# First layer of a two-layer hybrid transformer block: output product of head groups A and B once for all token tiles, root buffers by kind, and an FFN that opens with six blocks for the context alone

## The chip, the cores and the metric

The kernel runs on one core of a Trainium2 chip. A core has five engines that run their own instruction streams and meet at semaphores: TensorE (PE, matrix products), VectorE (DVE), ScalarE (ACT), GpSimd (POOL) and SyncE (SP, which here only issues transfers). The metric is the device time of one execution in microseconds. What can be told from no change is about 0.3%, that is 5.5 us.

## The reference

Two layers work on 256 context tokens and 256 latent tokens of width 1024. In both, a combined input product feeds three head groups (A: windowed attention, B: a state-space scan, C: differential attention), their outputs are joined and multiplied by `w_out`, and a layer norm follows; then a feed-forward network, dense in the first layer and with eight experts in the second, and another layer norm.

```python
for li in range(DEPTH):                                    # DEPTH = 2
    sh1, sc1, g1, sh2, sc2, g2 = split(c_act @ w_ada[li] + b_ada[li], 6)     # and ..c for the context
    ya, yb, yd = group_A(...), group_B(...), group_C(...)  # 384 + 384 + 256 columns
    mix = concat([ya, yb, yd], -1) @ w_out[li]
    x = post_ln(ALPHA * x + g1 * mix, ln1_g[li], ln1_b[li])
    x = post_ln(ALPHA * x + g2 * ffn(modulate(x, sh2, sc2)), ln2_g[li], ln2_b[li])
    # layer 0: the same for ctx, with the context's own sh, sc, g
# ffn of layer 0: g, u = split(h @ w_gu, 2); (silu(g) * u) @ w_down        # 1024 -> 2816 -> 1024
```

## The kernel before

The 512 tokens are four tiles of 128: tiles 0 and 1 are the context (`CTX`), 2 and 3 the latent tokens (`LAT`). Every large product is made from split operands: a weight piece `raw` is loaded (four buffers), ACT copies it into `whi` (a rounded form), and DVE or POOL subtracts to get `wlo` (three buffers each, function `split`); three products `hi*hi`, `hi*lo`, `lo*hi` are added up in one accumulator (`mm3`, lines 273, 274 and 276). Activations are split the same way into `HI` and `LO`.

In the first layer the end of attention, the output product and the start of the FFN overlap. Attention C makes for each head a pair of scores (`SC`, L919), a softmax on DVE and ACT, transposes (`PT`, L865), and a product with the values (`yC`, L932); when all heads of a tile are done DVE takes an inverse root by a chain of small instructions (`rstd_of`, L227 to L239) and scales (L942), and PE transposes the result (`py`, L952). `tail0` runs beside it. It calls `out_ab` (the columns of groups A and B times `w_out`, in four column blocks `j`, each with a weight piece of 512 KB and one of 256 KB) and `out_c` (the columns of group C), first for the context tiles and then for the latent ones, so the pieces of `out_ab` are loaded and split twice. After `out_c` of a tile come `post_ln` (L479, L480) and `layernorm` (`lnx`, L425), and for a pair of tiles `make_hT`: eight steps that transpose `lnx` (`hT`, L433) and write `HI` and `LO` of that half (L438 to L444), the input of the FFN.

Then `ada_group(L1, 0)` stands in the program: sixteen loads of 512 KB of `w_ada`, each followed by four products `ada` (L316; the profile counts two records for each) with the conditioning vector; the result is needed at the end of the FFN. It shares the four `raw` buffers. `ffn` follows: 22 column blocks in two halves; `gate_up(f, s)` loads 1 MB of weights for a block (two pieces, POOL makes the `wlo` of the first, DVE of the second) and makes 48 products `gu`, with 256 columns if `s` is one half of the tokens and with 512 if both. The first `M0` = 3 blocks run for the context half alone, then the same three for the latent half, and the other eight of the first half for both.

The order on every engine is not written out: a scheduler places each instruction, by the program's order, its dependencies and a timeline of its own, and engines then work strictly in that order. The constants of the second layer (`lcst`, L376) are loaded on SP into the buffer that the first layer's constants hold until attention C's last use of them (L935).

Of the kernel before, what the change touches and what calls it, by code (L numbers as in the profile page):

```python
# [12 lines left out]
F = mybir.dt.float32  # L13
FR = mybir.dt.float32r
BF = mybir.dt.bfloat16
I32 = mybir.dt.int32
# [15 lines left out]
FT = 22  # L32
NE = 8
BIG = 1.0e30
M0 = 3
LOP = 0, 1
KP = 1, 0
XC = 0, 4
# [76 lines left out]
def kernel(ctx: ExitStack, tc: tile.TileContext, I, out: bass.AP):  # L115
# [21 lines left out]
    def p_(tag, name):  # L137
        return ps.tile([128, 512], F, name=name, tag=tag, bufs=NBUF[tag])
# [79 lines left out]
        return (I["ctx"] if t in CTX else I["x"])[0, (t % 2) * 128:(t % 2 + 1) * 128]  # L218


    def rstd_of(v, n, scale=1.0):


        a = sm.tile([128, 3, 8], F, name="nw", tag="nw", bufs=6)
        ve, y, t = (a[:, i, :n] for i in range(3))
        iv = sm.tile([128, 2, 8], I32, name="nwi", tag="nwi", bufs=6)
        V.tensor_scalar(ve, v, scale, EPS, op0=OP.mult, op1=OP.add)  # L227
        V.tensor_scalar(iv[:, 0, :n], ve.bitcast(I32), 1, None, op0=OP.logical_shift_right)
        V.tensor_scalar(iv[:, 1, :n], iv[:, 0, :n], -1, 0x5F3759DF, op0=OP.mult, op1=OP.add)
        cur, f = iv[:, 1, :n].bitcast(F), 1.0  # L230
        for _ in range(3):
            if n == 1:
                V.scalar_tensor_tensor(t, cur, ve, cur, op0=OP.mult, op1=OP.mult)
            else:
                V.tensor_tensor(t, cur, cur, op=OP.mult)
                V.tensor_tensor(t, t, ve, op=OP.mult)
            V.scalar_tensor_tensor(y, t, 3.0 * f * f, cur, op0=OP.subtract, op1=OP.mult)
            cur, f = y, -2.0 * f ** 3
        V.tensor_scalar(y, y, 1.0 / f, None, op0=OP.mult)  # L239
        return y  # L240
# [178 lines left out]

    def layernorm(pool, xs, t):  # L420
        mu, rs = ln_stats(xs[t])
        n = pool.tile([128, D], F, name="lnx", tag="lnx", bufs=LNB if pool is lp else 4)
        nm = sm.tile([128, 1], F, name="nmr", tag="nmr")
        V.scalar_tensor_tensor(nm, mu, -1.0, rs, op0=OP.mult, op1=OP.mult)
        S.activation(n, xs[t], AF.Identity, scale=rs, bias=nm)  # L425
        return n
# [79 lines left out]
    def mixers(L, full_ctx, fill, tail):  # L506
# [326 lines left out]
        def ssd_finish(t, y):  # L833
            z = zcol(t, 0, 384)
            th = sp.tile([128, 384], F, name="zth", tag="yB", bufs=3)
            S.activation(r4(th, 3), z, AF.Tanh, scale=0.5)
            V.scalar_tensor_tensor(r4(th, 3), r4(th, 3), 1.0, z, op0=OP.add, op1=OP.mult)
            V.scalar_tensor_tensor(y, y, 0.5, th, op0=OP.mult, op1=OP.mult)
            ss = sm.tile([128, 1], F, name="ss", tag="ss")
            S.activation(th, y, AF.Square, accum_out=ss)  # L840
            rs = rstd_of(ss, 1, 1.0 / 384)
            V.scalar_tensor_tensor(y, y, rs, L.snw, op0=OP.mult, op1=OP.mult)
            put_y(t, y, 3, 3)

# [61 lines left out]
        def attn_C(t):  # L906
            n = keys(t)
            nb = n // 128
            y = mp.tile([128, 256], F, name="yC", tag="yCs", bufs=2)
            ss = sm.tile([128, 4], F, name="ssC", tag="ssC")  # L910
            for h in range(4):
                st_ = sm.tile([128, 5, 2], F, name="smx", tag="smx", bufs=6)
                l, r = st_[:, 2], st_[:, 3]
                Ps, pos = [], []
                for i in range(2):
                    po = p_("S", "SC")
                    pos.append(po)
                    b0 = 32 * ((2 * h + i) % 4)
                    T.matmul(po[:, :n], qTC(t)[b0:b0 + 32, h // 2], kTC[b0:b0 + 32, h // 2, :n], start=True,  # L919
                             stop=True)  # L920
                for i in range(2):
                    Ps.append(softmax(pos[i], n, None, 32 ** -0.5, st_, i))
                yield 0.0017 * n
                V.reciprocal(r, l)
                V.tensor_tensor(r[:, 1:2], r[:, 1:2], L.nlam, op=OP.mult)
                S.activation(Ps[1][:, :n], Ps[1][:, :n], AF.Copy, scale=r[:, 1:2])
                V.scalar_tensor_tensor(Ps[0][:, :n], Ps[0][:, :n], r[:, 0:1], Ps[1][:, :n], op0=OP.mult, op1=OP.add)
                PT = transp(Ps[0], n)
                yield 0.08 * nb
                yp = p_("y", "yC")  # L930
                for b in range(nb):
                    T.matmul(yp[:, 0:64], PT[:, b], vC[:, b, h * 64:(h + 1) * 64], start=(b == 0), stop=(b == nb - 1))  # L932
                yh = y[:, h * 64:(h + 1) * 64]
                S.activation(yh, yp[:, 0:64], AF.Square, accum_out=ss[:, h:h + 1])
                V.tensor_tensor(yh, yp[:, 0:64], L.dnw, op=OP.mult)  # L935
                yield 0.13 * nb
                if h % 2 and t in CH[li] or h == 3:
                    a = h - 1 if t in CH[li] else 0
                    n_ = h + 1 - a
                    rs = rstd_of(ss[:, a:h + 1], n_, 1.0 / 64)  # L940
                    yv = y[:, a * 64:(h + 1) * 64]
                    V.tensor_tensor(r4(yv, n_), r4(yv, n_), rs[:, :, None].to_broadcast([128, n_, 64]), op=OP.mult)  # L942
                    put_y(t, yv, 6 + a // 2, n_ // 2)
                    yield 0.2
                    yield f"+yC{t}{h // 2}"
# [181 lines left out]
            post_ln(xs[t], *L.ln1, LN1[t - 2] if L.li else None)  # L1127
            yield t

    def ffn(L, pp, done):  # L1130
        li = L.li
        xs = L.xs
        W = I["ffn_w_gu"][0].rearrange("(k p) (a n) -> p k a n", p=128, a=2)
# [3 lines left out]
        b = bc_load(L.pp, I["ln2_b"][li], L.nbc)  # L1137
        act = {}

        def gate_up(f, s):  # L1140
            wk = kpieces(lambda k0: [((slice(None), slice(None), a), W[:, k0:k0 + 4, a, f * 128:(f + 1) * 128])
                                     for a in range(2)], [128, 4, 2, 128])
            o = slice(s.start * 256, s.stop * 256)
            pg = [p_("S", "gu"), p_("mm", "gu")]
            for a in range(2):
                for k0 in range(0, KC, KG):
                    mm3(pg[a][:, o], [(wk(k)[0][:, a], wk(k)[1][:, a], HI[:, s, k], LO[:, s, k], True)
                                      for k in range(k0, k0 + KG)], k0 == 0, k0 + KG == KC)
            sl = L.pp.tile([128, 512], F, name="silu", tag="otmp", bufs=OT)
            S.activation(sl[:, o], pg[0][:, o], AF.Silu)  # L1150
            V.tensor_tensor(sl[:, o], sl[:, o], pg[1][:, o], op=OP.mult)
            if f not in act:
# [6 lines left out]
        for half in range(2):  # L1159
# [2 lines left out]

            for s in range(2):
                for f in range(f0, f0 + n0):
                    gate_up(f, slice(s, s + 1))
            for f in range(f0 + n0, f0 + 11):
                gate_up(f, slice(0, 2))
            for c, tiles in ((0, (0, 1, 2, 3)), (1, (0, 1, 2, 3))) if half == 0 else DN:
# [553 lines left out]
    def tail0():  # L1722
        yield "?S"
        pp = L0.pp = L0.tp = post.enter_context(tc.tile_pool(name="post0", bufs=1))
        out_consts(L0, range(NT), pp)
        ns = {}
        for tiles in TL0:
            yield from out_ab(L0, tiles, pp)
            for v in out_c(L0, tiles, pp):
                if type(v) is int:  # L1730
                    ns[v] = layernorm(pp, L0.xs, v)
# [10 lines left out]
                    yield v  # L1742

    mixers(L0, True, [ada_group(L0, 1), ada_group(L0, 2)], tail0())
    for _ in ada_group(L1, 0):
        pass
    with tc.tile_pool(name="ffn", bufs=1) as fp:
        ffn(L0, fp, lambda tiles: make_hT(L0.pp, L1.mod1, {t: layernorm(L0.pp, L0.xs, t) for t in tiles},
                                          tiles[0] // 2))
    post.close()  # L1750


# [61 lines left out]
```

## Time and profile before

| | us |
|---|---|
| median of 3 runs | 1819.82 (1815.51 to 1820.83) |
| the profiled execution | 1821.04 |
| its span in the trace | 1819.2 |
| PE busy in it | 1663.7 (91%) |
| DVE, ACT, POOL busy | 1154.5, 874.4, 321.9 |

The profile is of one execution. Its times count from the start of the span; 1.8 us of the execution lie around the span. A PE that is called busy need not be at full speed: the clock that the chip grants it is listed beside it, in shares of 2.4 GHz, and 0.50 is the lower level of 1.2 GHz. Idle time is put down to what ended it.

### The profile page before, as it was taken

To read this page: it belongs to the slowest core of one execution; us is meant where nothing else is said; L and a number is where in the kernel's file an instruction comes from. 1 tells how busy PE (TensorE), PEld (TensorE's weight loads), DVE (VectorE), ACT (ScalarE), POOL (GpSimd) and SP (SyncE) were. 2 spreads that over 40 slices of the span, in tenths; PEclk is the share of its full clock that TensorE was granted. 3 is DMA by queue.
4 is the path that set the end of the run, shared out by engine and by line. 5 is a ranking of instruction groups with operands and counts; after the bars stand their busy time and mean duration, and the time that the engine had idled before them with its cause. 6 is when DMAs were issued, how large, how long until landed. Compare 5 with 4: busy or idle time off the path is not lost.

```text
span 1819.2 us, 26372 instructions
## 1 busy us (share of the span) xinstructions
PE 1663.7 (91%) x9454; PEld 1244.2 (68%) x9454; DVE 1154.5 (63%) x2224; ACT 874.4 (48%) x1447; POOL 321.9 (18%) x254
## 2 busy tenths in 40 slices
PE   5898989887999999987999984899999999999995
PEld 2677657674988888876786672487686685784782
DVE  4673668658632343288587756288785586982895
ACT  3433545543622132335444652376673574772770
POOL 1221013334420022474232141000000000000000
PEclk8999998878999999999899996899999999999998
DMA  9327454328633233345676227999999999999995
GB/s 306 86 67 236 127 149 123 107 66 269 188 93 96 89 101 96 110 165 167 209 223 207 65 82 300 395 406 409 408 406 376 399 406 409 406 408 387 408 407 229
DMA packets 248153, 436.09 MB, mean 240 GB/s; under 512 B 15025, under 2 KB 166329, under 8 KB 248017
## 3 DMA queue, kind: packets, MB, share of 16 engines
q1 hardware_dynamic: 246096, 429.55, 66.2%
q0 software_dynamic: 1920, 4.81, 1.0%
q8 instruction: 76, 1.25, 0.3%
q14 instruction: 61, 0.49, 0.1%
HBM read 431.08 MB, written 3.23 MB: 239 GB/s over the span
## 4 chain that ended last, share of the span: by engine, by line
PE 77%; DMA 8%; DVE 7%; issue 2%; ACT 2%; POOL 0%; SPq 0%; ACTq 0%; DVEq 0%; POOLq 0%
PE mg L1369 6%; PE mu L1369 6%; PE mdn L1369 5%; PE gu L273 5%; PE gu L274 5%; PE gu L276 4%; DMA raw<-in_w_ada 4%; PE mu L1358 3%; PE mg L1358 3%; PE mdn L1358 3%; PE tok L276 2%; DMA mraw<-in_exp_w_gu 2%; PE ada L316 2%; PE tok L273 2%; PE SC L919 2%; PE tok L274 2%
## 5 line engine op out<-in xcount | busy, mean ns | idle before, releaser
L1349 DVE TENSOR_TENSOR mwl<-mraw,mwh 128x1024 fp32r<-128x1024 f32 (+1 forms) x350 | 389.4, 1160 | 37.2 <-ACT mwh L1348 20.2
L1348 ACT ACTIVATE mwh<-mraw 128x1024 fp32r<-128x1024 f32 (+1 forms) x350 | 337.8, 1013 | 61.4 <-PE mg L1369 22.9
L260 POOL TENSOR_TENSOR wlo<-raw,whi 128x1024 fp32r<-128x1024 f32 (+2 forms) x93 | 224.1, 2416 | 482.2 <-ACT whi L259 435.1
L259 ACT ACTIVATE whi<-raw 128x1024 fp32r<-128x1024 f32 (+2 forms) x168 | 168.2, 1004 | 237.3 <-PE dn L274 71.9
L260 DVE TENSOR_TENSOR wlo<-raw,whi 128x1024 fp32r<-128x1024 f32 (+2 forms) x75 | 90.5, 1206 | 144.1 <-ACT whi L259 142.8
L273 PE MATMUL gu<-HI,whi 128*128 128x512 f32 (+1 forms) x400 | 144.2, 369 | 2.3 <-ACT whi L259 2.3
L274 PE MATMUL gu<-LO,whi 128*128 128x512 f32 (+1 forms) x400 | 144.9, 369 | 0.0
L273 PE MATMUL tok<-whi,HI 128*128 128x256 f32 (+2 forms) x400 | 108.7, 301 | 5.4 <-ACT xin L550 4.3
L274 PE MATMUL tok<-whi,LO 128*128 128x256 f32 (+2 forms) x400 | 106.4, 295 | 5.2 <-DVE LO L444 5.1
L316 PE MATMUL ada<-raw,cT 128*32 128x256 f32 x768 | 75.5, 430 | 37.8 <-DMA raw<-in_w_ada 35.9
L276 PE MATMUL gu<-HI,wlo 128*128 128x512 f32 (+1 forms) x400 | 98.5, 368 | 0.0
L273 PEld LDWEIGHTS tok<-whi,HI 128*128 128x128 f32 x400 | 79.2, 199 | 14.9 <-issue 5.4
L273 PEld LDWEIGHTS gu<-HI,whi 128*128 128x128 f32 x400 | 75.7, 190 | 15.8 <-ACT whi L259 2.5
L274 PEld LDWEIGHTS tok<-whi,LO 128*128 128x128 f32 x400 | 79.3, 199 | 9.1 <-DVE LO L444 5.8
L274 PEld LDWEIGHTS gu<-LO,whi 128*128 128x128 f32 x400 | 76.1, 191 | 12.8
L276 PEld LDWEIGHTS gu<-HI,wlo 128*128 128x128 f32 x400 | 70.5, 189 | 12.9
L273 PE MATMUL dn<-whi,ah 128*128 128x512 f32 x176 | 70.3, 399 | 5.6 <-ACT whi L259 5.6
L276 PE MATMUL tok<-wlo,HI 128*128 128x256 f32 (+2 forms) x400 | 72.3, 299 | 1.9 <-DVE nw L227 1.9
L1369 PE MATMUL mg<-mwh,Xh 128*128 128x512 f32 x240 | 72.5, 383 | 1.7 <-ACT mwh L1348 1.6
L1369 PE MATMUL mdn<-mwh,mah 128*128 128x512 f32 x220 | 70.1, 400 | 0.9 <-ACT mwh L1348 0.9
L1369 PE MATMUL mg<-mwh,Xl 128*128 128x512 f32 x240 | 70.8, 376 | 0.0
L1369 PE MATMUL mu<-mwh,Xl 128*128 128x512 f32 x240 | 70.7, 376 | 0.0
(361 smaller groups left out, 3496.5 us busy)
## 6 DMA issues: line engine op xcount, KB each, us to landing
mraw<-in_exp_w_gu SPq DMA_DIRECT2D x128, 1024.0 KB, 15.8
mraw<-in_exp_w_down SPq DMA_DIRECT2D x88, 1024.0 KB, 15.6
mraw<-in_exp_w_gu SPq DMA_DIRECT2D x64, 768.0 KB, 13.8
raw<-in_w_ada SPq DMA_DIRECT2D x88, 512.0 KB, 4.8
raw<-in_ffn_w_gu SPq DMA_DIRECT2D x100, 256.0 KB, 3.4
raw<-in_w_in SPq DMA_DIRECT2D x38, 512.0 KB, 5.1
raw<-in_ffn_w_down SPq DMA_DIRECT2D x30, 512.0 KB, 3.7
E<-cscr POOLq DMA_DIRECT2D x12, 384.0 KB, 7.2
```

Source lines behind the costliest of these rows:

```text
L259: S.activation(hi, raw, AF.Copy)
L260: (eng or V).tensor_tensor(lo, raw, hi.bitcast(F), op=OP.subtract)
L273: T.matmul(o, ah, bh, start=start and i == 0, stop=False)
L274: T.matmul(o, *((ah, bl) if wa else (al, bh)), start=False, stop=False)
L276: T.matmul(o, *((al, bh) if wa else (ah, bl)), start=False, stop=stop and i == n - 1)
L316: T.matmul(pa[32 * j:32 * j + 32, hs], cT[:, k], w[j], start=(k == 0), stop=(k == KC - 1), tile_position=(0, 32 * j), skip_group_check=True)
L919: T.matmul(po[:, :n], qTC(t)[b0:b0 + 32, h // 2], kTC[b0:b0 + 32, h // 2, :n], start=True, stop=True)
L1348: S.activation(wh, raw, AF.Copy)
L1349: V.tensor_tensor(wl, raw, wh.bitcast(F), op=OP.subtract)
L1358: T.matmul(pc[:, :w], xh, wl[:, c * 512:c * 512 + w], start=False, stop=stop)
L1369: T.matmul(pc[:, :w], x, wh[:, c * 512:c * 512 + w], start=start and x is xh, stop=False)
```

## The change

Three parts. First, `tail0` calls `out_ab` once for all four tiles ahead of both `out_c`, so its weight pieces are loaded and split once, and no product of A or B starts before all tiles' group A and B outputs are there. Second, the buffers of the inverse roots are separate for group B, group C and the rest (three each, where six were shared); `lnx` has three buffers in place of four; the FFN's `silu` has two buffers of its own. Third, `M0` is 6, `ada_group(L1, 0)` is no longer ahead of the FFN but inside it, as `side`, after the six blocks of the context half; the half blocks take their accumulators from other tags.

```diff
-M0 = 3
+M0 = 6
...
-    def rstd_of(v, n, scale=1.0):
+    def rstd_of(v, n, scale=1.0, kind=""):
-        a = sm.tile([128, 3, 8], F, name="nw", tag="nw", bufs=6)
+        a = (lc if kind else sm).tile([128, 3, 8], F, name="nw", tag="nw" + kind, bufs=3)
-        iv = sm.tile([128, 2, 8], I32, name="nwi", tag="nwi", bufs=6)
+        iv = (lc if kind else sm).tile([128, 2, 8], I32, name="nwi", tag="nwi" + kind, bufs=3)
...
-        n = pool.tile([128, D], F, name="lnx", tag="lnx", bufs=LNB if pool is lp else 4)
+        n = pool.tile([128, D], F, name="lnx", tag="lnx", bufs=LNB if pool is lp else 3)
...
-            rs = rstd_of(ss, 1, 1.0 / 384)
+            rs = rstd_of(ss, 1, 1.0 / 384, "S")
...
-                    rs = rstd_of(ss[:, a:h + 1], n_, 1.0 / 64)
+                    rs = rstd_of(ss[:, a:h + 1], n_, 1.0 / 64, "C")
...
-        def gate_up(f, s):
+        def gate_up(f, s, tags=("S", "mm")):
-            pg = [p_("S", "gu"), p_("mm", "gu")]
+            pg = [p_(tag, "gu") for tag in tags]
...
-            sl = L.pp.tile([128, 512], F, name="silu", tag="otmp", bufs=OT)
+            sl = L.pp.tile([128, 512], F, name="silu", tag="silu", bufs=2)
...
-                    gate_up(f, slice(s, s + 1))
+                    gate_up(f, slice(s, s + 1), ("mm" if s else "S", "S"))
+                if s == 0 and half == 0:
+                    for _ in side:
+                        pass
...
+        yield from out_ab(L0, range(NT), pp)
         for tiles in TL0:
-            yield from out_ab(L0, tiles, pp)
             for v in out_c(L0, tiles, pp):
...
-    for _ in ada_group(L1, 0):
-        pass
```

Three places show how the order moves. On PE, between the last heads of attention C (tile 2, the products `yC` and the transposes `py`) and the first transposes `hT` of the FFN's input; after:

```order
L276 MATMUL op<-wlo,HI 128x512 x2
L932 MATMUL yC<-vC,PT 128x64 x4
L865 MATMUL PT<-cf,P 128x128 x8
L932 MATMUL yC<-vC,PT 128x64 x12
L952 MATMUL py<-cf,yC 128x128 x2
L433 MATMUL hT<-cf,lnx 128x128 x2
L273 MATMUL op<-whi,HI 128x512 x2
```

and before, from the same two products on:

```order
L276 MATMUL op<-wlo,HI 128x512 x2
L932 MATMUL yC<-vC,PT 128x64 x4
L865 MATMUL PT<-cf,P 128x128 x8
L273 MATMUL op<-whi,HI 128x256
L274 MATMUL op<-whi,LO 128x256
L273 MATMUL op<-whi,HI 128x256
```

The 144 products `op` of 256 columns (`out_ab` of the latent tiles) that stood between these heads' `yC` and behind them are now all further up; `ada`, which stood around `py`, is gone from here too.

On PE, the 64 products `ada`, which now follow the context half's six blocks `gu`; after:

```order
L276 MATMUL gu<-HI,wlo 128x256 x4
L316 MATMUL ada<-raw,cT 32x256 x12
L433 MATMUL hT<-cf,lnx 128x128 x2
L316 MATMUL ada<-raw,cT 32x256 x4
L433 MATMUL hT<-cf,lnx 128x128 x2
L316 MATMUL ada<-raw,cT 32x256 x16
L337 MATMUL tp<-cf,rows 128x128 x2
L316 MATMUL ada<-raw,cT 32x256 x32
L337 MATMUL tp<-cf,rows 128x128 x2
L273 MATMUL gu<-HI,whi 128x256
```

and before, the last of them, ahead of the first `gu`:

```order
L316 MATMUL ada<-raw,cT 32x256 x20
L433 MATMUL hT<-cf,lnx 128x128 x4
L316 MATMUL ada<-raw,cT 32x256 x4
L433 MATMUL hT<-cf,lnx 128x128 x2
L316 MATMUL ada<-raw,cT 32x256 x4
L433 MATMUL hT<-cf,lnx 128x128 x4
L316 MATMUL ada<-raw,cT 32x256 x8
L433 MATMUL hT<-cf,lnx 128x128 x4
L273 MATMUL gu<-HI,whi 128x256
```

They were spread over the end of the output product and the context's `hT`; now they stand in one place with two pairs of `hT` and no `gu` among them.

On SP, what is queued ahead of the second layer's constants `lcst`; after:

```order
L253 DMA raw<-in_w_out 128x2x512 x4
L253 DMA raw<-in_ffn_w_gu 128x4x128 x6
L351 DMA bc<-gscr 128x1024
L253 DMA raw<-in_ffn_w_gu 128x4x128 x4
L376 DMA lcst<-in_attn_sink 128x6
L376 DMA lcst<-in_dt_bias 128x12
```

and before:

```order
L253 DMA raw<-in_w_out 128x256
L253 DMA raw<-in_w_out 128x2x256
L253 DMA raw<-in_w_out 128x2x512 x2
L376 DMA lcst<-in_attn_sink 128x6
L376 DMA lcst<-in_dt_bias 128x12
```

Ten loads of FFN weights, five pieces, now stand between `w_out` and the constants. On DVE `lcst` (L398 to L403) stands among the instructions of tile 2's inverse root and of tile 1's layer norm, before and after.

## Rows read from the trace of the kernel before

**Rows 1.** Stretches: us, then busy us of each engine, clock, DMA share, GB/s

```profile
355.00:382.00 27.00, 21.57 (x75) 14.02 (x76) 16.93 (x68) 14.24 (x45) 4.08 (x4) 0.63 0.01 2
...
426.90:448.70 21.80, 13.78 (x113) 6.05 (x109) 18.31 (x65) 9.50 (x18) 6.03 (x6) 0.84 0.99 303
580.00:600.00 20.00, 20.00 (x88) 16.24 (x87) 4.37 (x4) 3.81 (x4) 0.00 (x0) 1.00 0.28 86
```

**Rows 2.** PE's waits, 300 to 450: who, for whom, us, times, longest

```profile
PE py L952 <- DVE yC L942: 9.2, 2, 5.5
PE ada L316 <- DMA raw<-in_w_ada: 4.7, 4, 1.6
PE op L276 <- DVE wlo L260: 3.2, 1, 3.2
```

**Rows 3.** Timeline of PE, attention C: start, us, instruction, idle before it

```profile
345.92 0.28 PE L273 MATMUL op<-whi,HI 128*128 128x256 f32 x1
346.04 0.28 PE L274 MATMUL op<-whi,LO 128*128 128x256 f32 x1
346.36 1.12 PE L919 MATMUL SC<-kTC,YT 32*128 32x512 f32 x2
...
355.02 0.88 PE L952 MATMUL py<-cf,yC 128*128 128x128 f32 x3 [5.50 <-DVE yC L942]
...
371.77 2.07 PE L919 MATMUL SC<-kTC,YT 32*128 32x512 f32 x2
...
382.00 0.88 PE L952 MATMUL py<-cf,yC 128*128 128x128 f32 x3 [3.67 <-DVE yC L942]
```

**Rows 4.** Timeline of DVE: the inverse roots of tile 1, and layer norm pieces

```profile
378.85 0.23 DVE L227 TENSOR_SCALAR nw<-ssC 128x4 f32<-128x4 f32 x2
...
381.43 0.63 DVE L942 TENSOR_TENSOR yC<-yC,nw 128x256 f32<-128x256 f32 x2
...
422.97 1.28 DVE L480 SCALAR_TENSOR_TENSOR xr<-xr,nw,bc 128x1024 f32<-128x1024 f32 x1
```

**Rows 5.** Timelines of DVE, POOL and ACT: the end of attention C

```profile
401.96 0.23 DVE L935 TENSOR_TENSOR yC<-yC,lcst 128x64 f32<-128x64 f32 x1 [0.60 <-ACT yC L934]
...
403.53 2.33 DVE L235 TENSOR_TENSOR nw<-nwi 128x4 f32<-128x4 f32 x1
...
403.42 2.42 POOL L260 TENSOR_TENSOR wlo<-raw,whi 128x1024 fp32r<-128x1024 f32 x1
...
415.85 0.36 DVE L942 TENSOR_TENSOR yC<-yC,nw 128x256 f32<-128x256 f32 x1
...
435.31 1.24 ACT L425 ACTIVATE lnx<-xr,nmr,nw 128x1024 f32<-128x1024 f32 x1 [11.03 <-DVE nmr L424]
```

**Rows 6.** Transfers issued 400 to 450: count, KB each, us to landing

```profile
raw<-in_w_ada SPq DMA_DIRECT2D x16, 512.0 KB, 5.1
...
lcst<-in_lam_k SPq DMA_DIRECT2D x1, 32.0 KB, 3.4
```

**Rows 7.** The tile lcst: who uses it, ns min/median/max, first and last start

```profile
L376 SPq DMA_DIRECT2D lcst<-in_attn_sink x1: 340/340/340, 402.2 to 402.2; - x1
...
L376 SPq DMA_DIRECT2D lcst<-in_lam_k x1: 327/327/327, 407.0 to 407.0; - x1
L398 DVE TENSOR_SCALAR lcst<-lcst x1: 159/159/159, 407.2 to 407.2; 128x6 f32<-128x6 f32 x1
```

**Rows 8.** Timelines of PE and ACT: hT, ada and the first gu

```profile
436.84 0.44 PE L433 MATMUL hT<-cf,lnx 128*128 128x128 f32 x2
...
437.20 0.56 ACT L438 ACTIVATE HI<-hT,mod 128x256 fp32r<-128x256 f32 x1 [0.65 <-PE hT L433]
437.67 0.56 ACT L440 ACTIVATE hfull<-hT,mod 128x256 f32<-128x256 f32 x1
...
443.92 1.90 PE L316 MATMUL ada<-raw,cT 128*32 128x256 f32 x16
...
448.70 0.39 PE L273 MATMUL gu<-HI,whi 128*128 128x256 f32 x1 [2.29 <-ACT whi L259]
```

More of the change, by code (lines that the diff above doesn't have):

```diff
@@ L1128, in out_c, with ffn @@
             yield t
-    def ffn(L, pp, done):
+    def ffn(L, pp, done, side):
         li = L.li
@@ L1744 @@
     mixers(L0, True, [ada_group(L0, 1), ada_group(L0, 2)], tail0())
-    for _ in ada_group(L1, 0):
-        pass
     with tc.tile_pool(name="ffn", bufs=1) as fp:
         ffn(L0, fp, lambda tiles: make_hT(L0.pp, L1.mod1, {t: layernorm(L0.pp, L0.xs, t) for t in tiles},
-                                          tiles[0] // 2))
+                                          tiles[0] // 2), ada_group(L1, 0))
     post.close()
```

## The prediction, made before the changed kernel was run

> **What bounds the kernel now.** I read the stretches first, then PE's waits, then the timelines between 345 and 449 us, where everything that the change moves lies. PE is the bound nearly everywhere: it is busy 20 of 20 us in the FFN at full clock, 88 products of 512 columns in 20 us, so 0.227 us each, and it is short of work only in the stretch from the output product to the first `gu` [rows 1]. There two things are to be seen. From 355 to 382 PE runs at 0.63 of its clock and is idle 5.4 us with the transfers all but silent (0.01); from 426.9 to 448.7 it is busy 13.8 of 21.8 us while the DMA engines are full (0.99) at 303 GB/s: that is `w_ada`. The waits say what ends last: twice the inverse root of attention C (9.2 us), four times a load of `w_ada` (4.7), once a `wlo` of the second `out_ab` (3.2) [rows 2]. So before, the loads of `w_ada` and the chain of DVE run side by side, and both hold up the FFN.
>
> **Part 1, `out_ab` once.** It takes away 3 MB of loads, eight copies on ACT and eight subtractions. PE loses nothing: the products are the same. Those loads stood in front of no one but in the wait of 3.2 us [rows 2], so the saving is that, plus the idle time that the latent products can now fill.
>
> How much of it they fill: a product of 256 columns takes 0.118 us (345.92 to 346.04) [rows 3]. In the new order 216 of the 288 products stand ahead of the first `py` of group C, against 144 before, so 72 x 0.118 = 8.5 us of work go into an idle time of 5.5 [rows 3]: the first `py` comes 3.0 later. Then 28 stand between this `py` and the next heads' `PT`, and 20 between `PT` and `yC`: 48 x 0.118 = 5.7, of which some 1.8 were spent there before, so these heads are 6.9 late. Up to the second `py` (382.0 before; I call this point P) the other 24 products lie in waits. Against that, PE should be warmer: a pair of `SC` takes 1.12 us at full clock and 2.07 at the low one, and the last idle 3.7 us before P [rows 3] were DVE's; I take 5 us back. Last, the inverse root of tile 1: 2.6 us from L227 to L942, 13 pairs of instructions by 0.2, and 0.6 for L942 itself [rows 4]. In the new order tile 0's layer norm stands among them, L480 by 1.28 [rows 4], two statistics instructions at about half that and a dozen small ones by 0.1 to 0.2: 4.5 us more. P moves from 382 to 382 + 6.9 - 5 + 4.5, 388 rounded; bounds 381 (all of the clock and of the idle time is won back) and 393 (none).
>
> From P to `hT`, the first place that the order shows. Before, it takes 54.8 us (to 436.84) [rows 8], since DVE works off the latent products' and layer norms' instructions in between and lnx of tile 1 is only made at 435.31 [rows 5]. After, PE has there 12 products of 512 columns, 16 `PT`, 16 `yC` and two `py`, some 8 us, and then waits. DVE's chain is what counts: the last L935, tile 2's inverse root, tile 1's layer norm. Among these stand the `lcst` instructions, as before, where L398 started at 407.2, just 5.0 after its load was issued [rows 7]. In the new order that load stands behind five pieces of FFN weights, and the fifth needs the buffer of the first, which POOL must have subtracted: after tile 1's products (P + 7 if the clock is low), a copy, and a queue on POOL of two subtractions by 2.42 [rows 5] and an addition, that is P + 12, about when the last L935 ends too. Then 0.7 for the two loads of that piece, 5.0 to landing, 4.8 from the first constant's issue to the last one's [rows 7], 3.4 to its landing [rows 6]: L403 at P + 21, L480 and L942 at P + 23, where it took 14.2 us from L935 to L942 before [rows 5] and takes 11 now. Tile 1's layer norm then needs 4.7 us of small instructions and lnx 1.24 [rows 5]: `hT` at P + 29.7. So `hT` comes at 388 + 29.7 = 417.7 in place of 436.8. Bounds for this stretch: 24 (the constants land before DVE gets to them) and 33.
>
> **A rule on DVE and POOL.** The row first: an L235 of four columns, 0.1 us elsewhere, took 2.33 while POOL made a `wlo` of 2.42 [rows 5]. The Trainium skill, SBUF — State Buffer, section SBUF: two separate sides, says that DVE, in some modes or with two SBUF inputs, and GpSimd take turns on a shared pair of ports by an exclusive lock held for the whole instruction. The trace agrees in that row. By the rule the two subtractions that POOL makes after P could each hold DVE's chain for up to 2.4 us, 4.8 together; without it they cost nothing there, since DVE waits for the constants then. I take none and leave it to the upper bound.
>
> **Part 2, the buffers.** Three buffers for each kind in place of six for all: in a chain that one engine executes in order, nobody in the trace waits for them; nothing. The third `lnx` buffer is reused after the context's `hT`, which the order has ahead anyway; nothing. Two `silu` buffers serve blocks of 5.7 us; nothing. If this cover is gone, a wait of ACT's lnx, 1.24 us [rows 5], is the size.
>
> **Part 3, the FFN's opening.** The eight steps of `hT` are paced by ACT, two instructions by 0.47 us each [rows 8], 7.5 us; three copies of weights stand among them and wait for `out_c`'s products, so `HI` and `LO` are complete some 14 us after the first `hT`, and the first block ends 18.5 after it. Before: first `gu` at 448.7 [rows 8], 16 at the low clock, 32 at 0.118, end at about 456.2, that is 19.4 after. So the first block ends at 417.7 + 18.5 = 436.2 against 456.2: 20.0 us won.
>
> Half blocks: 48 x 0.118 = 5.66 us, full ones 48 x 0.227 = 10.90. Three more blocks in halves: 3 x (2 x 5.66 - 10.90) = +1.3. The latent `hT` wait for a layer norm whose instructions stand on DVE among the blocks' own: 0 to 5, taken 1.5 with the clock after the waits.
>
> Now `ada`, the second place. Its PE work is small (two loads' worth in 1.90 us, part of it at the low clock) [rows 8]; its loads are 8.4 MB. Four buffers let four of them land during the last context blocks. The other twelve are issued one by one as PE is done with a buffer, and nothing else stands on PE meanwhile. At 303 GB/s [rows 1], rounded up to 317 for the part that is only `w_ada`, a load takes 1.65 us; four in flight by 5.1 us to landing [rows 6] and 0.9 for use and issue give 1.5. So 12 x 1.65 = 19.8 us, 0.6 at the start, and at the end a piece of FFN weights behind the last loads, its copy on ACT and the first `gu`: 3.5. The stretch costs 24 us. Before, it cost what lies inside 426.9 to 448.7, which is already in the 456.2. Bounds: 18 and 27.
>
> The Trainium skill, DMA: Bandwidth & Descriptors, section Bandwidth, gives 341 GB/s for 1 MB in one transfer and 425 for 16 MB; by the higher figure twelve loads would take some 15 us (an estimate from that page) and the stretch 19. The row at a DMA share of 0.99 [rows 1] speaks for less, and the sum goes by it.
>
> **The sum.** - 20.0 + 24 + 1.3 + 1.5 = + 6.8, against the profiled execution's 1821.04: 1827.8. That execution is 1.2 above the median 1819.8, so 1826.5 for a median. The second layer's order changes a little and its work not at all; nothing.
>
> **Rivals.** *It comes out even:* both waits are a few us shorter than I have them, the constants land in time (24 in place of 29.7 from P) or the loads of `w_ada` flow faster (20 in place of 24). Each alone gives 1821 to 1822.5. For it: both prices are the least certain. Against it: the constants' landing and the full DMA are in rows.
>
> *Faster:* the clock. The latent products fill PE's idle time and attention C runs at full clock: the 21.6 busy us from 355 to 382 at 0.63 [rows 1] would be 13.6. Then P is at 380 in place of 388, the tail and `hT` are 4 shorter, and the latent `hT` don't wait (1.5): 1826.5 - 13.5 = 1813. For it: half of what bounds P is PE at the low clock. Against it: between heads DVE and ACT need their own time, and the products stand in front of them. It decides the sign if P is at 380 or earlier.
>
> *Much slower:* the latent `hT` come 5 late, ports lock DVE, P is at 393: + 5 + 5, 1836 to 1838.
>
> **How the numbers follow.** Chances: my forecast 0.48 (1826.5; 1823 to 1832), even 0.25 (1821.5), faster 0.18 (1813), much slower 0.09 (1837). What a measurement can tell from no change is 5.5 us: faster is below 1814.4, slower above 1825.3. Of the forecast's 0.48 some 0.1 lies within, of the even case's all but 0.02 on each side, of the faster case's 0.18 some 0.03: faster 0.17, same 0.33, slower 0.50. Range 1811 to 1836.
>
> **What would show it.** In the changed kernel's profile: no wait for `wlo` of the output product; the second `py` of group C at 384 to 391; PE idle most of the 15 us behind it, with L398 to L403 in DVE's row at the time the constants land; the first `hT` near 418; `ada` in one stretch of 18 us or more with waits for `raw<-in_w_ada` of some 10 us, where they were 4.7. Wrong it would be if `ada` took under 18 us, or if `hT` came before 410.

## The result, and the profile of the changed kernel

The changed kernel took 1831.2 us (median of 6, 1830.0 to 1838.6), the kernel before in the same comparison 1817.9 (1810.7 to 1820.8): a ratio of 1.0079, 95% interval 1.0056 to 1.0102. It is slower by some 14 us. Forecast was 1826.5, range 1811 to 1836. The profiled execution took 1830.0, 9.0 more than the profiled one of before.

Where the time went is read as before: stretches, waits, timelines. Stretches of the changed kernel first (us; busy us of PE, its weight loads, DVE, ACT, POOL; clock, DMA share, GB/s):

```profile
355.00:382.00 27.00, 24.26 (x145) 17.61 (x143) 16.98 (x45) 16.65 (x46) 15.19 (x12) 1.00 0.26 78
382.00:412.00 30.00, 13.19 (x67) 11.20 (x68) 17.90 (x96) 8.25 (x22) 8.28 (x6) 0.62 0.22 63
465.80:493.00 27.20, 16.54 (x137) 4.14 (x136) 2.74 (x9) 3.93 (x8) 1.45 (x2) 0.59 0.91 282
580.00:600.00 20.00, 20.00 (x88) 16.14 (x87) 6.11 (x6) 4.97 (x6) 0.00 (x0) 1.00 0.23 71
```

Attention C from 355 to 382 now runs at full clock (0.63 before, [rows 1]) and PE is busy in it 24.3 of 27 us. The low clock has moved behind it, to 382 to 412 (0.62 there, 0.90 in the same stretch before). The third row is new: from 465.8 to 493.0 PE does hardly anything but `ada`. The same kernel's PE waits from 300 to 500 (total, times, longest):

```profile
PE py L952 <- DVE lcst L407: 9.0, 1, 9.0
PE ada L316 <- DMA raw<-in_w_ada: 8.9, 11, 1.6
PE py L952 <- DVE yC L942: 6.3, 1, 6.3
PE gu L274 <- DVE nwi L228: 3.9, 1, 3.9
```

The wait for `wlo` is gone; that for `w_ada` went from 4.7 us to 8.9 [rows 2]. Its timeline of PE, cut to the places the prediction named (start, us, instruction, idle before it):

```profile
354.93 0.49 PE L952 MATMUL py<-cf,yC 128*128 128x128 f32 x3
...
381.98 0.99 PE L932 MATMUL yC<-vC,PT 128*128 128x64 f32 x4 [1.09 <-DVE yC L935]
...
389.27 0.88 PE L952 MATMUL py<-cf,yC 128*128 128x128 f32 x3 [6.30 <-DVE yC L942]
...
412.03 0.66 PE L952 MATMUL py<-cf,yC 128*128 128x128 f32 x2 [8.96 <-DVE lcst L407]
...
417.71 0.38 PE L433 MATMUL hT<-cf,lnx 128*128 128x128 f32 x2
...
428.13 0.58 PE L274 MATMUL gu<-LO,whi 128*128 128x256 f32 x1 [3.85 <-DVE nwi L228]
...
465.74 1.50 PE L316 MATMUL ada<-raw,cT 128*32 128x256 f32 x24
...
490.08 1.08 PE L316 MATMUL ada<-raw,cT 128*32 128x256 f32 x8 [0.99 <-DMA raw<-in_w_ada]
493.02 0.58 PE L273 MATMUL gu<-HI,whi 128*128 128x256 f32 x1 [0.56 <-ACT whi L259]
```

The first `py` of group C is where it was (354.9, 355.0 before). P is at 389.3, tile 1's `hT` at 417.7, and `ada` takes the 27.3 us from 465.7 to 493.0. Counted on the timeline, the 48th `gu` of 256 columns, the end of block 0, is at 435.1; before it was at 456.4. The first `dn` starts at 584.8 (575.3 before). So the opening is 21.3 us earlier, all that and 9.5 more is given back by the first `dn`, and the rest of the program, 1243 us, moves this by 0.6.

### The profile page after: what moved, and what is told of

Its sections match the earlier page's. It is cut to its first block, busy times and chain, and to the rows that moved or that the text cites. A ratio compares the mean times of both kernels' runs of the same rounds, so it can differ in the third digit from the quotient of the medians.

```text
span 1828.1 us, 26675 instructions
## 1 busy us (share of the span) xinstructions
PE 1662.7 (91%) x9598; PEld 1247.5 (68%) x9598; DVE 1156.5 (63%) x2229; ACT 875.2 (48%) x1451; POOL 322.2 (18%) x253
## 4 chain that ended last, share of the span: by engine, by line
PE 74%; DVE 9%; DMA 9%; issue 2%; ACT 2%; POOL 0%; SPq 0%; ACTq 0%; DVEq 0%; POOLq 0%
PE mg L1372 6%; PE mu L1372 6%; PE mdn L1372 5%; PE gu L274 4%; PE gu L273 4%; PE gu L276 4%; DMA raw<-in_w_ada 4%; PE mg L1361 3%; PE mu L1361 3%; PE mdn L1361 3%; PE ada L316 2%; DMA mraw<-in_exp_w_gu 2%; PE tok L273 2%; PE tok L276 2%; PE tok L274 2%
## 5 line engine op out<-in xcount | busy, mean ns | idle before, releaser
L259 ACT ACTIVATE whi<-raw 128x1024 fp32r<-128x1024 f32 (+2 forms) x166 | 168.0, 1013 | 253.8 <-PE dn L274 70.8
L274 PE MATMUL gu<-LO,whi 128*128 128x512 f32 (+1 forms) x448 | 151.4, 351 | 4.2 <-DVE nwi L228 3.9
L273 PE MATMUL gu<-HI,whi 128*128 128x512 f32 (+1 forms) x448 | 150.1, 350 | 0.6 <-ACT whi L259 0.6
L274 PEld LDWEIGHTS gu<-LO,whi 128*128 128x128 f32 x448 | 86.4, 194 | 15.3 <-DVE LO L444 4.1
L273 PEld LDWEIGHTS gu<-HI,whi 128*128 128x128 f32 x448 | 86.2, 194 | 12.0 <-ACT whi L259 1.0
L276 PEld LDWEIGHTS gu<-HI,wlo 128*128 128x128 f32 x448 | 75.5, 192 | 10.9
L1372 PE MATMUL mu<-mwh,Xh 128*128 128x512 f32 x240 | 70.8, 376 | 0.0
```

What stands on the lines that cost most here:

```text
L259: S.activation(hi, raw, AF.Copy)
L273: T.matmul(o, ah, bh, start=start and i == 0, stop=False)
L274: T.matmul(o, *((ah, bl) if wa else (al, bh)), start=False, stop=False)
L276: T.matmul(o, *((al, bh) if wa else (ah, bl)), start=False, stop=stop and i == n - 1)
L1372: T.matmul(pc[:, :w], x, wh[:, c * 512:c * 512 + w], start=start and x is xh, stop=False)
```

## The experiments

All lengths that the following speaks of stand in one table, read from the timeline of each kernel's trace: P is the second `py` group of attention C, *heads* the last part of P, from the first `py` of group C to P, *opening* from P to the end of block 0, *FFN* from there to the first `dn`, *down* from the first to the last `dn` piece, *rest* from there to the end of the span.

| kernel | P | heads | opening | FFN | down | rest | ratio to before (95%) |
|---|---|---|---|---|---|---|---|
| before | 382.0 | 27.0 | 74.4 | 118.9 | 254.0 | 989.9 | |
| before, again | 379.9 | 25.2 | 72.5 | 118.9 | 253.8 | 990.2 | |
| changed | 389.3 | 34.3 | 45.8 | 149.7 | 253.8 | 989.5 | 1.0079 (1.0056 to 1.0102) |
| changed, again | 391.7 | 34.3 | 45.9 | 147.2 | 255.5 | 987.1 | |
| `ab_twice` | 387.0 | 27.2 | 55.4 | 150.5 | 253.8 | 994.3 | 1.0079 (1.0049 to 1.0110) |
| `ab_only` | 387.9 | 34.4 | 56.5 | 124.3 | 254.7 | 994.0 | 0.9993 (0.9968 to 1.0018) |
| `ada_ahead` | 391.5 | 39.2 | 49.6 | 124.5 | 255.7 | 990.8 | 0.9969 (0.9945 to 0.9993) |
| `half3` | 391.2 | 34.4 | 45.6 | 145.4 | 253.7 | 987.5 | 1.0036 (1.0014 to 1.0058) |
| `old_bufs` | 391.5 | 37.7 | 51.8 | 148.2 | 253.0 | 989.2 | 1.0102 (1.0065 to 1.0138) |
| `lcst2` | 392.9 | 34.3 | 45.6 | 148.1 | 255.2 | 991.7 | 1.0101 (1.0061 to 1.0142) |
| `woven` | 383.0 | 34.4 | 45.5 | 138.6 | 254.4 | 997.3 | 1.0005 (0.9981 to 1.0030) |
| `woven`, again | 385.4 | 34.4 | 45.5 | 138.1 | 254.5 | 994.3 | |
| `woven_full` | 388.6 | 34.5 | 45.7 | 131.7 | 258.1 | 996.4 | 0.9996 (0.9974 to 1.0018) |
| `ada_split` | 395.8 | 37.6 | 46.8 | 127.3 | 253.9 | 993.5 | 0.9983 (0.9958 to 1.0008) |

**How far single traces can be compared.** The changed kernel and the kernel before, once more each.

> The changed kernel once more, for a second trace of the same order. Theory: where it starts late is a matter of the execution (the granted clock before attention C's tail), where it is slow is a matter of the order. So P may lie anywhere in 382 to 393, but P to the end of block 0 is 45.7 within 0.5, from there to the first dn 149.7 within 1.5, and from the last dn piece to the end 989.5 within 2. Rival: these lengths too differ by 4 us or more between executions, and then single traces can't be compared at all.

> The kernel before once more. Theory: P to the end of block 0 74.4 within 1, from there to dn 118.9 within 1, from the last dn piece to the end 989.9 within 2, while P may differ from 382.0 by 5 us. Rival: as for the changed kernel, lengths differ by 4 us or more.

P row of the changed kernel's second trace, then of before's:

```profile
391.71 0.87 PE L952 MATMUL py<-cf,yC 128*128 128x128 f32 x3 [6.37 <-DVE yC L942]
```

```profile
379.87 0.87 PE L952 MATMUL py<-cf,yC 128*128 128x128 f32 x3 [3.68 <-DVE yC L942]
```

The lengths hold: opening 45.8 and 45.9, FFN 149.7 and 147.2 (wider than the 1.5 expected), rest within 2.4; of before 74.4 and 72.5, 118.9 twice, 989.9 and 990.2. P does not hold. Six traces (changed twice, `woven` twice, `half3`, `woven_full`) have one and the same order of PE up to the opening's first `gu`, and in them P lies anywhere from 383.0 to 391.7, 388.2 on average. All of that spread lies ahead of the first `py`: from it to P the six take 34.3 to 34.5, where before takes 27.0 and 25.2. So lengths are compared to 2 or 3 us, *heads* among them, and a P only as a mean.

**Which part loses, which part gains.** The two parts apart: `ada` ahead of the FFN again with all else changed; `out_ab` once as the only change; and `out_ab` twice with all else changed.

```diff
 # ada_ahead
+    for _ in ada_group(L1, 0):
+        pass
     with tc.tile_pool(name="ffn", bufs=1) as fp:
-        ... ada_group(L1, 0))
+        ... ())
 # ab_only (on the kernel before)
+        yield from out_ab(L0, range(NT), pp)
         for tiles in TL0:
-            yield from out_ab(L0, tiles, pp)
 # ab_twice
-        yield from out_ab(L0, range(NT), pp)
         for tiles in TL0:
+            yield from out_ab(L0, tiles, pp)
```

> The changed kernel with one thing undone: the second layer's first ada group stands ahead of the FFN again. Theory: the earlier opening of the FFN comes from the output product taken once, and the loss from ada's own stretch of 27.2 us (465.8 to 493.0) and the first block behind it at the low clock (2.6 us). With ada ahead, its sixteen loads run from about 385 on beside attention C's tail, where the DMA engines are nearly idle, and PE's products of ada fill PE's waits there; the FFN's weights come behind them, which I take to cost 5 us at the opening. 1831 - 27 - 3 + 5 = 1806, range 1800 to 1812. Rival: the opening comes early only because ada is gone from there; then the opening falls back towards 449 and the time is 1818 to 1824.

> The kernel before with one part of the change alone: out_ab once for all four tiles (three half blocks, ada ahead of the FFN, buffers as they were). Theory: the same as for ada ahead, with three blocks fewer in halves (1.3 us less): 1805, range 1799 to 1812. Rival (this part gives nothing without ada's move): 1815 to 1822, no difference from before.

> The changed kernel with out_ab again called once for the context and once for the latent tiles; ada stays inside the FFN. Theory: ada's stretch, the cold block and three more split blocks cost 31 us as in the changed kernel, and the opening wins only what ada's traffic took from it, 5 to 10 us: 1818 + 31 - 8 = 1841, range 1836 to 1848. Rival (the opening is won by ada's move): 1828 to 1833, as the changed kernel.

`ada`'s place is the loss. With it ahead the first `dn` comes at 565.5, inside at 584.8 and 584.9: 19.3 us, and the whole execution is 1.1% (20 us) shorter, clear of both intervals. (Of the 19.3, 2.7 and, in the second trace, 5.1 us lie ahead of the first `py`, where PE's order is the same, so the traces alone show 14 to 17.) It is also the one version here whose interval lies below the kernel before, by 0.3%, about the least that can be told. But it was expected 8 us shorter still. What it costs ahead shows in its stretch from 374 to 409 and in its PE waits from 375 to 465:

```profile
374.00:409.00 35.00, 27.50 (x207) 14.45 (x205) 19.52 (x81) 8.92 (x25) 9.53 (x8) 0.76 0.81 251
```

```profile
PE py L952 <- DVE nw L239: 9.1, 1, 9.1
PE ada L316 <- DMA raw<-in_w_ada: 4.7, 5, 1.4
PE hT L433 <- ACT lnx L425: 2.1, 2, 1.5
```

The loads flow from 374 on beside attention C's tail, as the theory has it, at 251 GB/s; but some of their products stand ahead of P and wait there (*heads* 39.2 in place of 34.3), the opening is 3.8 us longer, and among the latent half blocks an `hT` waits 1.5 us for its layer norm. So `ada` ahead costs 8.7 us up to the end of block 0, and inside the FFN it costs 23 to 25 more than ahead.

`out_ab` once alone gave no difference in total, against the 1805 expected. It does what it was to do, the opening is 16 to 18 us shorter than before (56.5), but it pays with *heads* (7 to 9 longer), with 5 us in the FFN and with 4 in the rest. In the FFN PE waits 3.5 us for the `LO` of the latent half, where before it waited for nothing; that three context blocks are too few to cover this is my reading, and was not tried. `ab_twice` has an opening 9.6 us longer than the changed kernel, but *heads* of 27.2, as before, so 7.1 shorter: up to the end of block 0 `out_ab` once is worth only 2.5 us beside the other parts. That is within what single traces can tell, and the total is the same within some 5 us either way (its median of 1835.8 lies below the theory's range and above the rival's). So the gain of that part beside the others is not shown: it takes from the opening what it mostly puts ahead of P.

**The size of the cover.** Half blocks three instead of six.

```diff
-M0 = 6
+M0 = 3
```

> The changed kernel with M0 = 3 in place of 6: ada's stretch stands behind three half blocks of the context. Theory: P to the end of block 0 stays 45.8 us, from there to the first dn 149.7 - 1.3 = 148.4, the time 1830, range 1826 to 1834. Rival: with ada three blocks earlier some of the latent products and hT (some 4 us of PE) fall into ada's waits in place of the blocks, so 144 from block 0 to dn and 1826.

FFN took 145.4, between the two expectations and nearer the rival (144); the ratio is 0.4% lower than the changed kernel's, the two intervals just touching. In `ada`'s stretch stand 16 `hT` (4.0 us of PE) where the changed kernel has four (0.9), so `hT` do fall into `ada`'s waits, as the rival has it; products `op` do not. But against the changed kernel's second trace (147.2) the FFN is only 1.8 shorter, 1.3 of it the theory's, so which of the two it is can't be told from the lengths. `ada`'s own stretch is 25.6 us there, so its length does not hang on what stands ahead.

**The buffers.**

```diff
-        a = (lc if kind else sm).tile(..., tag="nw" + kind, bufs=3)     # nwi alike
+        a = sm.tile(..., tag="nw", bufs=6)
-        n = pool.tile(..., tag="lnx", bufs=LNB if pool is lp else 3)
+        n = pool.tile(..., tag="lnx", bufs=LNB if pool is lp else 4)
-            sl = L.pp.tile(..., tag="silu", bufs=2)
+            sl = L.pp.tile(..., tag="otmp", bufs=OT)
```

> The changed kernel with the buffers as before: six shared for the inverse roots, four for lnx, silu with otmp. Theory: the buffers give and take nothing; P to the end of block 0 45.8, from there to dn 149.7, each within 1 us, the time 1831, range 1827 to 1835. Rival: the shared root buffers hold a chain back at the end of attention C, P to the end of block 0 is longer by 1.2 us or more, and the time is 1833 or more.

The rival holds for the opening: it is 6 us longer, 51.8, and *heads* are 3.4 longer (37.7). The context tiles' layer norms on ACT, tile 0's and tile 1's, with the old buffers and then in the changed kernel:

```profile
416.49 1.24 ACT L425 ACTIVATE lnx<-xr,nmr,nw 128x1024 f32<-128x1024 f32 x1 [2.41 <-DVE nmr L424]
...
430.04 1.24 ACT L425 ACTIVATE lnx<-xr,nmr,nw 128x1024 f32<-128x1024 f32 x1 [6.82 <-DVE nmr L424]
```

```profile
391.02 1.24 ACT L425 ACTIVATE lnx<-xr,nmr,nw 128x1024 f32<-128x1024 f32 x1
...
415.95 1.24 ACT L425 ACTIVATE lnx<-xr,nmr,nw 128x1024 f32<-128x1024 f32 x1 [2.39 <-DVE nmr L424]
```

With the old buffers both come later, by 25 and by 14 us, since DVE makes their sums later, tile 1's among a latent tile's. PE's `hT` of tile 1 waits for that:

```profile
PE hT L433 <- ACT lnx L425: 9.0, 1, 9.0
```

`ab_only`, which has the old buffers too, shows the same wait of 9.1 us. Between 380 and 450 no wait in either trace is for a reader of one of these buffers, so the chain is not held back as the rival thought; what differs is the order in which DVE's instructions are placed. Which of the three changes of buffers does it was not tried. In total 1.0102 can't be told from 1.0079.

**The constants.** A second buffer for `lcst`, so that the second layer's constants are there long before.

```diff
-        k = lc.tile([128, 640], F, name="lcst", tag="lcst", bufs=1)
+        k = lc.tile([128, 640], F, name="lcst", tag="lcst", bufs=2)
-            sl = L.pp.tile([128, 512], F, name="silu", tag="silu", bufs=2)
+            sl = L.pp.tile([128, 512], F, name="silu", tag="otmp", bufs=OT)
```

> The changed kernel with a second buffer for the layer constants lcst (room for it comes from silu using otmp's buffers), so that the second layer's constants are loaded long before and none stands in DVE's chain at the end of attention C. Theory of the prediction: they hold that chain. In the changed kernel's trace L942 comes 8.0 us behind the last L935, with DVE's idle time of about 2.5 us around L398 to L403; without them I expect 5 to 6 us from L935 to L942, the third py at P + 19 to 20 in place of P + 22.8, block 0 ends at P + 42.5 in place of P + 45.8, and the time is 1828, range 1822 to 1832. Rival: the chain is DVE's own work and the constants fill gaps in it; then L935 to L942 stays within 0.5 us of 8.0 and block 0 ends at P + 45.8.

DVE's chain in the changed kernel, then without constants in it:

```profile
403.45 0.23 DVE L935 TENSOR_TENSOR yC<-yC,lcst 128x64 f32<-128x64 f32 x1 [1.70 <-ACT yC L934]
...
408.23 0.17 DVE L401 TENSOR_SCALAR lcst<-lcst 128x12 f32<-128x12 f32 x1 [1.86 <-ACT lcst L400]
409.35 0.19 DVE L402 TENSOR_SCALAR lcst<-lcst 128x64 f32<-128x64 f32 x1
410.13 0.22 DVE L403 TENSOR_TENSOR lcst<-lcst 128x64 f32<-128x64 f32 x1
...
411.47 0.42 DVE L942 TENSOR_TENSOR yC<-yC,nw 128x256 f32<-128x256 f32 x1
```

```profile
407.95 0.22 DVE L935 TENSOR_TENSOR yC<-yC,lcst 128x64 f32<-128x64 f32 x1 [1.24 <-ACT yC L934]
...
414.18 0.37 DVE L942 TENSOR_TENSOR yC<-yC,nw 128x256 f32<-128x256 f32 x1
```

The chain itself is as the theory had it, 6.2 us instead of 8.0 (the one row with idle time for constants has 1.86). The opening is not: 45.6 against 45.8. Tile 2's heads, ahead of the chain, ended 0.9 later from P, and what follows the third `py` took 0.8 longer. So the constants are in the chain and worth 2 us there, and nothing at the end of block 0. The total, expected at 1828, came out at a ratio of 1.0101, no shorter than the changed kernel.

**Spreading `ada`.** Two loads with their products behind each latent half block and the first full ones (`woven`, also a second time), behind the full blocks and the first down product (`woven_full`), and half of them ahead, half behind full blocks (`ada_split`).

```diff
                 for f in range(f0, f0 + n0):
-                    gate_up(f, slice(s, s + 1), ("mm" if s else "S", "S"))
-                if s == 0 and half == 0:
-                    for _ in side:
-                        pass
+                    gate_up(f, slice(s, s + 1))
+                    if s:                        # woven only
+                        next(side, 0)
             for f in range(f0 + n0, f0 + 11):
                 gate_up(f, slice(0, 2))
+                if half == 0:
+                    next(side, 0)
 # woven_full: the same line also ahead of each piece of the first down product
 # ada_split: four steps of ada_group ahead of the FFN, the others behind the full blocks
```

`woven` and `woven_full` thereby also go back to the half blocks' accumulators of before; `ada_split` keeps the changed ones. The accumulators were not tried alone.

> The changed kernel with ada not in one stretch: two of its loads with their products behind each latent half block and behind the first two full blocks. Theory: the stretch is a wait for loads, so spread over blocks that PE is busy in it costs only its products, 128 by 0.068 at full clock = 8.7 us in place of 27.2, and the cold block (2.6) is gone: 1831 - 21 = 1810, range 1805 to 1816. Rival: with four shared buffers two loads of 512 KB more for each half block of 5.7 us (2 MB in 6.7 us, 313 GB/s) are more than the DMA engines gave in the stretch (273 to 290), so PE waits at each half block for 1 us or two and half of the gain is lost: 1818 to 1824.

> The changed kernel with ada woven in later and more thinly: two of its loads behind each of the five full blocks of the first half, the rest among the pieces of the first down product. In the version woven behind the half blocks ada cost 18.2 us from block 0 to the first dn, 11.6 of it PE busy with ada, and half blocks took 8 us in place of 5.7. Theory: the rest was loads waiting in half blocks, where the weights alone ask for 185 GB/s; in full blocks they ask for 96. So 131 us from the end of block 0 to dn where the changed kernel has 149.7, 3 to 4 more in the first down product, and the second layer as it may come (its order changes): 1831 - 15 = 1816, range 1810 to 1821. Rival: ada's products cost the blocks around them as much here (18 us): 1819 to 1824, as woven.

> The version with ada woven behind the half blocks once more. From the last dn piece to the end its first trace has 997.3 us where the changed kernel has 989.5. Theory: the second layer is placed anew by the scheduler after every change and its order costs these 7 us; then it is 995 or more again. Rival: it is the clock of that one execution; then it is 992 or less.

> A version meant to be faster: the changed kernel with half of ada (eight loads) ahead of the FFN and the other half behind four of the full blocks. Theory: ada ahead held the opening by 4 us (P to the end of block 0 49.7 in place of 45.7) and P by some 3, and woven ada costs its products, 5.8 for half of it, and little waiting. So P to the end of block 0 47.5, from there to dn 120 + 6 + 3 = 129: 17 to 19 us less than the changed kernel, 0.996 to 0.999 of the kernel before, no worse than ada ahead (0.997). Rival: half of the loads hold P and the weights as much as all sixteen did (49.7 or more), and the time is that of the kernel before or 0.2% above.

Stretches of `woven`: its six latent half blocks, then its full ones; and in the same stretches `ada` alone (busy us of PE first):

```profile
458.70:507.40 48.70, 45.38 (x387) 38.16 (x386) 18.43 (x25) 20.17 (x34) 14.28 (x8) 1.00 0.79 236
507.40:566.80 59.40, 59.40 (x288) 46.39 (x287) 17.99 (x20) 18.44 (x24) 12.01 (x5) 1.00 0.52 157
```

```profile
458.70:507.40 48.70, 8.65 (x88) 2.62 (x88) 0.43 (x1) 1.00 0.79 236
507.40:566.80 59.40, 2.99 (x40) 0.89 (x40) 0.42 (x1) 1.00 0.52 157
```

The clock stays at 1.00 and PE waits 3.3 us in all, so spreading takes some 10 us off the FFN (149.7 and 147.2 to 138.6 and 138.1), half of what was expected. The products are dearer than thought, 11.6 us of PE, not 8.7. In the full blocks it goes better: 131.7, where 131 was expected, and 4 us in the down product, as expected. `ada_split` is at 127.3, and its opening at 46.8. Yet none of the three ends clearly below the kernel before, and `woven` and `woven_full`, with medians of 1821.2 and 1822.0, took what their rivals said: the *rest* of `woven` is 997.3 and 994.3 and that of `woven_full` 996.4, where the changed kernel has 989.5 and 987.1. Repeating `woven` gave 994.3, just short of the 995 set for the theory and above the rival's 992. The second layer's instructions are placed anew with every change ahead of them, but that this order costs 7 us is not shown. From the last `dn` piece to the end `lcst2` has the same order of PE as `woven`, and its rest is 991.7. The first 200 us of that in `woven`, then in `lcst2`:

```profile
822.00:1022.00 200.00, 186.42 (x1319) 146.67 (x1318) 146.62 (x356) 95.54 (x201) 54.81 (x63) 0.91 0.58 180
```

```profile
842.00:1042.00 200.00, 186.11 (x1368) 147.02 (x1367) 150.59 (x370) 97.17 (x210) 55.69 (x62) 0.95 0.59 181
```

One order of PE thus gives 991.7 to 997.3; at a clock of 0.91 in place of 0.95 `woven` gets through fewer products (1319 records, not 1368) in the same busy time. So not all of those 7 us are the order's; whether any are stays open. In `ada_split` eight loads still held P: *heads* are 37.6 in its one trace, 3.2 more than in the changed kernel.

## Why the prediction came out as it did

**P.** Forecast 388; the mean of the six traces is 388.2, against 382.0 and 379.9 before. That it fits is luck: by its terms misses cancel. The first `py` was to come 3.0 later and came where it was (354.9, 355.0 before). DVE's chain was to cost 4.5 more: the wait ahead of P went from 3.7 to 6.3, so 2.6. The rest of the heads, between the first `py` and P, was to cost 3.9 less 5 from the clock: the clock did rise, to 1.00, but with 145 records in place of 75 PE was busy 24.3 of 27 us, and they cost 4.7.

**From P to `hT`.** L403 was forecast at P + 21 and came at P + 20.9, L942 at P + 23 and came at P + 22.2, tile 1's `hT` at P + 29.7 and came at P + 28.4. Here too misses cancel: the last L935 was to come at P + 12 and came at P + 14.2, and from it to L942 it took 8.0 us, not 11. (The first pair of `hT`, at 412.5, belongs to tile 0, which I had not set apart.) The reason given, constants landing late, is only a part of it: without them 1.8 us of the chain go, and the opening stays. The even case, whose price for constants in time was 5.7 us, had no ground there.

**Block 0.** Forecast 18.5 us behind tile 1's `hT`, at 436.2; measured 17.4 and 435.1, so 21.3 us won where I had 20.0.

**DVE and POOL.** I counted nothing for the two engines holding each other up. (The L235 that I compared with takes 0.15 to 0.16 us elsewhere in that trace, not 0.1.) They did, behind the stretch that I had in mind, and it lengthens PE's wait of 3.85 us at 428.13. DVE in the changed kernel, an L479 of 1.28 us in its undisturbed place, its own `wlo`, and the L479 and L444 that PE waits for, then POOL's `wlo` alone and beside it:

```profile
404.70 1.28 DVE L479 SCALAR_TENSOR_TENSOR xr<-xr,mv,bc 128x1024 f32<-128x1024 f32 x1
...
421.71 1.69 DVE L260 TENSOR_TENSOR wlo<-raw,whi 128x1024 fp32r<-128x1024 f32 x1
...
423.98 2.70 DVE L479 SCALAR_TENSOR_TENSOR xr<-xr,mv,bc 128x1024 f32<-128x1024 f32 x1
426.60 1.48 DVE L444 TENSOR_TENSOR LO<-hfull,HI 128x256 fp32r<-128x256 f32 x1
```

```profile
395.67 2.38 POOL L260 TENSOR_TENSOR wlo<-raw,whi 128x1024 fp32r<-128x1024 f32 x1 [3.63 <-ACT whi L259]
...
422.27 3.33 POOL L260 TENSOR_TENSOR wlo<-raw,whi 128x1024 fp32r<-128x1024 f32 x1
```

L479 took 1.42 longer, POOL's `wlo` 0.95; POOL's `wlo` began while DVE's ran (to 423.40), and L479 began while POOL's ran (to 425.60). The Trainium skill, SBUF — State Buffer, section SBUF: two separate sides, has the two engines take turns on shared ports, each for a whole instruction; these rows agree within 0.2 us, and each engine pays in its turn. Of PE's 3.85 us that is 1.4 for L479 and up to 1.1 for L444 (0.42 at its next place, 428.79); the remainder I put down to the place of these instructions in DVE's order. It is inside the 17.4 us above, so the sum did not suffer.

**`ada`'s stretch** is the term that was mis-sized: 24 us forecast, bound 27, measured 27.3 and, in five other traces with such a stretch, 25.6 to 27.4. The loads were to come every 1.65 us; the last twelve came every 1.92 (23.0 us from 468.2 to 491.2, where 19.8 were forecast), and in the others every 1.74 to 1.90. The start took 2.5 us, not 0.6 (32 records of `ada` and two pairs of `hT` stand in it), and the end 1.8, not 3.5. The 23.0 us of the twelve loads:

```profile
468.20:491.20 23.00, 13.47 (x100) 2.79 (x100) 1.09 (x4) 1.41 (x4) 0.72 (x1) 0.56 0.97 305
```

The row's 303 GB/s came again, so it should have been taken as it stood, not rounded up to 317; and `w_ada` had only 273 of the 305, since the first weights of the next block, issued from 485.4 on, flow among the last loads. The Trainium skill, DMA: Bandwidth & Descriptors, section Bandwidth, gives 341 GB/s for 1 MB in one transfer; these loads of 512 KB stay below that: one every 1.92 to 1.74 us is 273 to 301 GB/s.

**Clock and split blocks.** 1.5 was put down for the latent `hT` and the clock behind `ada`. The first latent block took 8.3 us (493.0 to 501.3) in place of 5.7, its row at a clock of 0.69 where full blocks have 1.00, so 2.6.

**The sum.** -21.3 to the end of block 0 and +30.8 in the FFN (27.3 `ada`, 2.6 the cold block, 1.3 the split blocks, less 0.4) make +9.5, where the forecast had +6.8. With the 0.6 that went again behind it the profiled execution is 9.0 longer, 2.2 more than forecast. The other 2.3 of the 4.7 us between 1826.5 and 1831.2 are the base: the profiled execution of the changed kernel lies 1.1 below its median, and I had set it 1.2 above, as before's was.

**Part 2, the buffers: nothing.** That was wrong as a price, by 6 us in the opening and 3.4 ahead of P. The total did not suffer, since I had read the place of `hT` from the changed order, which has the buffers in it; I only put the gain down to part 1.

**Rivals.** The faster case had the clock right (1.00) and the time wrong: P was never at 380 with this order: from the first `py` to P it took 34.3 to 34.5 us although the clock was 1.00 up to 382, where 27.0 had been enough at 0.63; the latent products in between took the place of the idle time. The much slower case's P of 393 did not come in this order either.

## What to carry to other kernels

Loads that cost little beside an idle engine cost their full time once they stand where that engine is otherwise busy: price moved work by what else its new place could do. Before moving it, ask whether the wait it shared was its own: here, from the first `py` to the end of block 0, all parts together won 17 to 21 us, `ada`'s move gave some 9 of them, and then cost 23 to 25 in the FFN. And count from a mark that the change does not move: the opening alone, counted from P, looks 27 to 29 us shorter, but 7 to 9 of them only went ahead of P. Last, where a scheduler places the instructions, a change of buffers or of one loop can re-place everything behind it; compare lengths between fixed marks in two traces of each kernel before a few us are given a cause.

## What the runs showed of the hardware

Six traces of one order differ in P by 8.7 us. All of it arises ahead of the first `py`, and it goes with the granted clock: from 150 to 340 us, where their instructions are the same, that was 0.95 in the changed kernel's second trace (P at 391.7) and 1.00 in `woven` (383.0):

```profile
150.00:340.00 190.00, 182.05 (x1338) 135.15 (x1337) 115.15 (x349) 93.29 (x258) 36.23 (x26) 0.95 0.46 143
```

```profile
150.00:340.00 190.00, 181.41 (x1362) 133.90 (x1361) 120.94 (x360) 95.52 (x262) 39.06 (x29) 1.00 0.46 144
```

The other four lie in the same order: 0.96 with 391.2, 0.98 with 389.3 and 388.6, 1.00 with 385.4. Why the clock is granted differently to the same work was not found out. I had taken P of one trace as a property of the kernel; it is one to 4 or 5 us either way.
